# Weight sums of the second feed-forward layer: 28 pairs summed by VectorE in 8 KB rows in place of accumulating transfers

## The chip, the cores and the metric

The kernel runs on one core of a Trainium2 chip. The metric is the device time of one execution in microseconds (us). A run's time is the median of several executions; beside it stands one profiled execution, from which every row of a view below is taken. In those rows PE is TensorE, DVE is VectorE, ACT is ScalarE, POOL is GpSimd and SP is SyncE, which issues most of the transfers (SPq is its queue). L154 is line 154 of the kernel.

## What is computed

The reference is an encoder trunk of two layers on x of 256 positions by 2048 channels, all in float32. Layer 0 mixes by pooling and grouped-query attention, layer 1 by a bidirectional mLSTM of eight heads of width 256. Each layer then has a gated feed-forward part:

```python
def conv_ffn(x, w_up, conv_w, conv_b, w_down):
    u = x @ w_up                      # 256 x 2048 by 2048 x 11264
    up = jnp.pad(u, ((0, 0), (1, 1), (0, 0)))
    u = c[0] * up[:, :-2] + c[1] * up[:, 1:-1] + c[2] * up[:, 2:] + conv_b
    gate, val = jnp.split(u, 2, axis=-1)
    return (jax.nn.silu(gate) * val) @ w_down
```

The mLSTM layer projects x to queries, keys, values and an output gate (`h @ w_in`), computes for each head a 256 by 256 matrix of weighted scores, multiplies it with the values, and projects back with `w_out`.

## The kernel before

**The weight stream.** All weights pass through one stream (class `Stream`, L66 to L175) of 904 tiles of 128 partitions by 1024 floats, numbered from w0. The mLSTM layer's tiles are w404 to w565, the second feed-forward layer begins at w566. A tile is loaded by SP (`load`, L83; plain tiles at L100), then split into two float32r parts, high and low, called hl with the same number (`split`, L147): ScalarE copies the high part (L153) and VectorE subtracts it from the raw tile (L154). TensorE multiplies with high and low parts in three matmuls per product. Loads run six tiles ahead of TensorE in the mLSTM layer and eight in the feed-forward layers, splits three and four (`st.la`, `st.sa`). There are seven raw buffers and five split buffers: the load of a tile waits for the split of the tile seven before it, and a split waits until TensorE has done with the tile five before it.

**The order of work.** TensorE's program order is written by hand. The matrix products of the stream follow each other, and short tasks (`Weave`, L176) are put between them after a set amount of TensorE work. The other engines' order is made when the kernel is built: a scheduler puts their instructions in the order in which its own model of time has them ready; an instruction of an engine waits for those ahead of it on that engine.

**One head of the mLSTM** (`head`, L834) is such a task. VectorE prepares the gate matrix `arg` (L843), TensorE multiplies queries and keys into `qk`, VectorE multiplies the two (L856) and makes a divisor `denr` (L859 to L861), then four instructions write the matrix `A` (L863 to L866). TensorE transposes A (`atr`, L872), ScalarE and VectorE split the result into `at` (L874, L875), TensorE multiplies it with the values (`av`). The head's key tile is `hl_k` (L823), written by VectorE before `qk`.

**Summed weights.** Part of each up-projection is done with seven products of half-size blocks instead of eight, for units of four column tiles listed in `UNITS` (L1252). Those products need sums of weight blocks. For a pair of row tiles the four blocks b11, b12, b22, b21 lie side by side in DRAM, 512 floats each, 8 KB per partition in all. Four sums are made: s1 = b11 + b12, s2 = b12 + b22, s3 = b22 + s1, s4 = b21 + s3. A unit has eight pairs. The last number of its entry in `UNITS` is its kind. Kind 2, which most units have, makes s1, s3 and s4 ahead of time in a DRAM buffer G: SP copies blocks from DRAM to G (L122, L124), GpSimd issues transfers that add into G (L125 for s1, L129 for s3 and s4). s2 is then made by VectorE when the tile comes by (kind "left" of a tile, L141). Kind 1 makes all four ahead.

**When the sums are made.** `make_step` (L112) does one of four steps of a pair. `_make_steps` (L1339) gives each pair a place in the stream, "at", and a gap: step 0 comes right after the load of tile "at", step n after n gaps more. The second layer has 48 pairs, in the order of `UNITS`: 24 of the units (1,1), (2,1), (3,0), then those of (3,1), (4,1), (5,1). The first 28 pairs had these places (L1445), where `at` is 566:

```python
[(at - 240 + 11 * k, 5) for k in range(7)] + [(at - 162 + 38 * k // 5, 4) for k in range(21)]
```

Seven pairs were thus made during the first feed-forward layer, 21 during the mLSTM layer; the other 20 are made in the second feed-forward layer.

## Time and profile before

| | |
|---|---|
| median of 3 runs | 2157.26 us (2156.75 to 2157.31) |
| the profiled execution's own time | 2156.8 us |
| its span, first to last instruction | 2155.0 us |
| TensorE busy | 2148.3 us (100%) |
| VectorE busy | 1733.2 us (80%) |
| ScalarE busy | 1322.3 us (61%) |
| GpSimd busy | 301.7 us (14%) |
| SP's and ACT's transfers (queue q1) | 544.01 MB, 71.3% of 16 engines' time |
| GpSimd's transfers (queue q0) | 65.30 MB, 19.9% |

The median is 0.5 us above the profiled time, and the profiled time is 1.8 us above its span. A row of a timeline gives the start in us, the length in us, engine, line, operation, the tile written and the tiles read (without their numbers), a count where several equal instructions are merged, and in brackets how long the engine was idle before it and what released it.

### The profile page before, as it was taken

How to read it: one execution, taken by the hardware profiler on the slowest of the kernel's cores; microseconds unless marked ns; L12 is line 12 of the kernel's file. 1: busy time of each engine (PE TensorE's matmuls, PEld its weight loads, DVE VectorE, ACT ScalarE, POOL GpSimd, SP SyncE). 2: the span in 40 equal slices, each digit the busy share in tenths (PEclk: the TensorE clock that was granted, in tenths of full speed). 3: DMA queues.
4: the chain of work that ended last, by engine and by line, in shares of the span. 5: the costliest groups of instructions: out<-in, count | busy, mean ns of one | idle time of the engine just before them, and what ended most of it. 6: DMA issues, size and time to landing. Idle time of an engine off the chain costs nothing.

```text
span 2155.0 us, 31044 instructions
## 1 busy us (share of the span) xinstructions
PE 2148.3 (100%) x10824; PEld 1821.3 (85%) x10824; DVE 1733.2 (80%) x2417; ACT 1322.3 (61%) x1856; POOL 301.7 (14%) x376
## 2 busy tenths in 40 slices
PE   9999999999999999999999999999999999999999
PEld 8888888888888888889888888888888888888887
DVE  7686698989889787866777677669898979888985
ACT  7665566766557566656454544456676757675763
POOL 0222111111111111111111111111111111100000
PEclk9999999999999999999999999999999999999999
DMA  9989889999999999979898888888999999998773
GB/s 354 254 227 255 255 251 355 304 346 317 308 331 315 347 325 338 318 213 264 237 268 247 253 247 255 258 245 237 328 332 331 324 323 349 325 313 261 253 249 106
DMA packets 213727, 615.03 MB, mean 285 GB/s; under 512 B 27354, under 2 KB 29698, under 8 KB 213570
## 3 DMA queue, kind: packets, MB, share of 16 engines
q1 hardware_dynamic: 173216, 544.01, 71.3%
q0 software_dynamic: 37280, 65.30, 19.9%
q10 hardware_dynamic: 3074, 3.75, 0.7%
q8 instruction: 84, 1.38, 0.2%
q14 instruction: 73, 0.60, 0.1%
HBM read 610.81 MB, written 132.16 MB: 345 GB/s over the span
## 4 chain that ended last, share of the span: by engine, by line
PE 98%; DVE 1%; issue 0%; ACT 0%; DVEq 0%; ACTq 0%
PE up L282 22%; PE dn L282 22%; PE p L282 19%; PE op L282 8%; PE mv L282 4%; PE mq L282 4%; PE mk L282 4%; PE mo L282 4%; PE qproj L282 3%; PE pool L282 1%; PE kproj L282 1%; PE vproj L282 1%; PE tr L1097 1%; DVE hl L154 1%; PE av L282 1%; PE qk L282 1%
## 5 line engine op out<-in xcount | busy, mean ns | idle before, releaser
L154 DVE TENSOR_TENSOR hl<-w,hl 128x1024 fp32r<-128x1024 f32 (+1 forms) x904 | 1089.5, 1219 | 302.1 <-ACT hl L153 287.0
L153 ACT CAST hl<-w 128x1024 fp32r<-128x1024 f32 (+2 forms) x903 | 935.9, 1048 | 623.0 <-DVE w L141 105.2
L282 PE MATMUL up<-xx,hl 128*128 128x512 f32 (+1 forms) x2816 | 513.7, 337 | 0.0
L282 PEld LDWEIGHTS up<-xx,hl 128*128 128x128 f32 x2816 | 446.3, 188 | 70.4
L282 PE MATMUL dn<-hl,g 128*128 128x512 f32 x2064 | 492.1, 391 | 0.0
L282 PEld LDWEIGHTS dn<-hl,g 128*128 128x128 f32 x2064 | 385.3, 188 | 79.1
L282 PE MATMUL p<-hl,sx 128*128 128x512 f32 x1056 | 280.0, 390 | 0.2 <-DVE hl L154 0.2
L125 POOL DMA_DIRECT2D G<-in_q x176 | 148.1, 847 | 800.8 <-DMA G<-in_q 800.8
L282 PEld LDWEIGHTS p<-hl,sx 128*128 128x128 f32 x1056 | 193.6, 188 | 37.6 <-DVE hl L154 0.5
L129 POOL DMA_DIRECT2D G<-G x160 | 140.4, 882 | 605.4 <-DMA G<-in_q 266.8
L282 PE MATMUL p<-hl,xx 128*128 128x512 f32 x792 | 216.2, 390 | 0.0
L282 PEld LDWEIGHTS p<-hl,xx 128*128 128x128 f32 x792 | 144.6, 188 | 27.2
L282 PE MATMUL mk<-xx,hl 128*128 128x512 f32 (+1 forms) x512 | 92.2, 338 | 0.0
L282 PE MATMUL mq<-xx,hl 128*128 128x512 f32 (+1 forms) x512 | 92.2, 337 | 0.0
L282 PE MATMUL mv<-hl,xx 128*128 128x512 f32 (+2 forms) x480 | 91.8, 350 | 0.0
L282 PE MATMUL op<-hl,cat 128*128 128x512 f32 x384 | 91.6, 393 | 0.0
L282 PE MATMUL mo<-hl,xx 128*128 128x512 f32 x384 | 90.5, 391 | 0.0
L282 PE MATMUL op<-hl,mcat 128*128 128x512 f32 x384 | 89.5, 392 | 0.0
L282 PEld LDWEIGHTS mq<-xx,hl 128*128 128x128 f32 x512 | 79.3, 188 | 11.6
L282 PEld LDWEIGHTS mk<-xx,hl 128*128 128x128 f32 x512 | 79.1, 188 | 11.4
L282 PEld LDWEIGHTS mv<-hl,xx 128*128 128x128 f32 x480 | 78.3, 189 | 11.2
L282 PEld LDWEIGHTS op<-hl,mcat 128*128 128x128 f32 x384 | 71.5, 188 | 14.6
(242 smaller groups left out, 1877.8 us busy)
## 6 DMA issues: line engine op xcount, KB each, us to landing
w<-in_up SPq DMA_DIRECT2D x176, 512.0 KB, 6.6
w<-in_dn SPq DMA_DIRECT2D x176, 512.0 KB, 6.3
w<-in_m_in SPq DMA_DIRECT2D x124, 512.0 KB, 5.8
w<-in_q SPq DMA_DIRECT2D x96, 512.0 KB, 7.4
G<-in_q SPq DMA_DIRECT2D x160, 256.0 KB, 6.5
G<-G POOLq DMA_DIRECT2D x160, 256.0 KB, 7.4
w<-G SPq DMA_DIRECT2D x80, 512.0 KB, 7.2
w<-in_a_in SPq DMA_DIRECT2D x46, 512.0 KB, 6.5
```

Of the source, the lines that this page charges most:

```text
L125: pin(add.dma_start(G[r, 0:512], src[r, 512:1024], accum_op=ALU.add))
L129: pin(add.dma_start(G[:, at : at + 512], G[:, of : of + 512], accum_op=ALU.add))
L153: (self.nc.vector.tensor_copy if i + c == 0 else self.nc.scalar.copy)(hl[:, 0, c : c + n], w[:, c : c + n])
L154: self.nc.vector.tensor_sub(hl[:, 1, c : c + n], w[:, c : c + n], hl[:, 0, c : c + n].bitcast(F32))
L282: pe.matmul(out_, lhsT, rhs, start=start, stop=stop, skip_group_check=True)
L1097: pe.transpose(tr[:, j, t * P : t * P + P], src[:, c : c + P], ident)
```

## The change

Unit entries (1,1), (2,1) and (3,0) of the second layer become kind 1, so that s2 of their 24 pairs is made ahead too and no longer by VectorE when the tile comes by; that tile is then loaded in two halves, one from G and one from the weights. The first 28 pairs get a new kind 4, made in three steps: SP loads the pair's 8 KB rows (1 MB) into an SBUF room; one tile later VectorE makes the four sums in place; five or six tiles after the load SP stores the room (1 MB) to G. There are three rooms: two lie in the buffer that the mLSTM layer later uses as mcat1, one, gm, is new. The first 20 pairs take the rooms in turn, one pair every 4.25 tiles; the last eight pairs all use gm, one every eight tiles. All 28 pairs are made in the mLSTM layer. The memory set aside for GpSimd's transfers is halved, which makes place for gm.

```diff
         self.made, self.make, self.dpool = {}, make, dpool
+        self.rooms, self.room = [], {}
...
-        if part < 2:
+        if kind == 4:
+            if part == 0:
+                self.room[key] = self.rooms.pop(0)
+                pin(sync.dma_start(self.room[key], src))
+            elif part == 1:
+                w, sum_ = self.room[key], self.nc.vector.tensor_add
+                b11, b12, b22, b21 = (w[:, j * 512 : j * 512 + 512] for j in range(4))
+                pin(sum_(b11, b11, b12))
+                pin(sum_(b12, b12, b22))
+                pin(sum_(b22, b22, b11))
+                pin(sum_(b21, b21, b22))
+            else:
+                pin(sync.dma_start(G, self.room.pop(key)))
+        elif part < 2:
...
-            catb = [actp.tile([P, 8, 2, S], F32R, tag=f"B{i}", name=f"mcat{i}") for i in range(2)]
+            catb = []
+            gm = kp.tile([P, 2048], F32, tag="gm", name="gm")
+            gb = actp.tile([P, 2, 2048], F32, tag="B1", name="gb")
+            st.rooms = ([gb[:, 0], gb[:, 1], gm] * 7)[:20] + [gm] * 8
...
+                while len(catb) <= k // 8:
+                    catb.append(actp.tile([P, 8, 2, S], F32R, tag=f"B{len(catb)}", name=f"mcat{len(catb)}"))
+                    assert len(catb) < 2 or len(st.rooms) < 9
...
-    ((1, 1, 17, 37, 2), (2, 1, 38.5, 59, 2), (3, 0, 60, 79, 2), (3, 1, 80, 97, 2), (4, 1, 98.5, 121, 2),
+    ((1, 1, 17, 37, 1), (2, 1, 38.5, 59, 1), (3, 0, 60, 79, 1), (3, 1, 80, 97, 2), (4, 1, 98.5, 121, 2),
...
-    for (key, kind, q), (at, gap) in zip(pairs, places):
-        for part in range(4):
-            make.setdefault(at + part * gap, []).append((key, kind, part, q))
+    for (key, kind, q), (at, *gaps) in zip(pairs, places):
+        steps = [gaps[0] * part for part in range(4)] if len(gaps) == 1 else [0, *gaps]
+        for part, gap in enumerate(steps):
+            make.setdefault(at + gap, []).append((key, kind if len(gaps) == 1 else 4, part, q))
...
-    nc = _bacc.Bacc("TRN2", target_bir_lowering=False, num_devices=1, dynamic_dma_scratch_size=4096)
+    nc = _bacc.Bacc("TRN2", target_bir_lowering=False, num_devices=1, dynamic_dma_scratch_size=2048)
...
-    places.append([(at - 240 + 11 * k, 5) for k in range(7)] + [(at - 162 + 38 * k // 5, 4) for k in range(21)]
+    places.append([(at - 152 + 17 * k // 4, 1, 6) for k in range(20)] + [(at - 63 + 8 * k, 1, 5) for k in range(8)]
```

TensorE's order of instructions is the same in both kernels. On VectorE, ScalarE and SP the order changes, at many places of the mLSTM layer. Three of them follow; in the changed kernel all lines below the middle of `make_step` have higher numbers (L154 becomes L168, L859 becomes L879, L863 becomes L883).

The first place is VectorE at head 1. qk1, den1, denr1 and A1 are that head's tiles, hl437 to hl439 the split tiles of the stream, gb and gm the rooms. Before:

```order
L856 SCALAR_TENSOR_TENSOR arg1_9853,den1_9916<-qk1_9903,arg1_9853 128x128
L859 SCALAR_TENSOR_TENSOR denr1_9921<-den1_9916 128x4
L860 TENSOR_TENSOR denr1_9921<-denr1_9921,mc_9456 128x4
L861 RECIPROCAL denr1_9921<-denr1_9921 128x4
L863 TENSOR_SCALAR A1_9925<-arg1_9853,denr1_9921 128x256
L865 TENSOR_SCALAR A1_9925<-arg1_9853,denr1_9921 128x256
L864 SCALAR_TENSOR_TENSOR A1_9925<-arg1_9853,denr1_9921,A1_9925 128x128
L866 SCALAR_TENSOR_TENSOR A1_9925<-arg1_9853,denr1_9921,A1_9925 128x128
L154 TENSOR_TENSOR hl438_9974<-w438_9882,hl438_9974 128x1024
```

and in the changed kernel:

```order
L876 SCALAR_TENSOR_TENSOR arg1_9791,den1_9851<-qk1_9838,arg1_9791 128x128
L127 TENSOR_TENSOR gm_8968<-gm_8968 128x512
L126 TENSOR_TENSOR gb_8969<-gb_8969 128x512
L879 SCALAR_TENSOR_TENSOR denr1_9856<-den1_9851 128x4
L168 TENSOR_TENSOR hl438_9916<-w438_9821,hl438_9916 128x1024
L127 TENSOR_TENSOR gb_8969<-gb_8969 128x512
L880 TENSOR_TENSOR denr1_9856<-denr1_9856,mc_9387 128x4
L881 RECIPROCAL denr1_9856<-denr1_9856 128x4
L168 TENSOR_TENSOR hl439_9933<-w439_9865,hl439_9933 128x1024
L883 TENSOR_SCALAR A1_9860<-arg1_9791,denr1_9856 128x256
L885 TENSOR_SCALAR A1_9860<-arg1_9791,denr1_9856 128x256
L884 SCALAR_TENSOR_TENSOR A1_9860<-arg1_9791,denr1_9856,A1_9860 128x128
```

Before, the writes of A1 stood ahead of the splits hl438 and hl439; now both splits and three sums stand ahead of them.

The second place is VectorE at head 7, near the end of the layer. Before:

```order
L154 TENSOR_TENSOR hl533_12525<-w533_12440,hl533_12525 128x1024
L856 SCALAR_TENSOR_TENSOR arg7_12428,den7_12492<-qk7_12479,arg7_12428 128x128
L856 SCALAR_TENSOR_TENSOR arg7_12428,den7_12492<-qk7_12479,arg7_12428 128x256 x2
L856 SCALAR_TENSOR_TENSOR arg7_12428,den7_12492<-qk7_12479,arg7_12428 128x128
L859 SCALAR_TENSOR_TENSOR denr7_12497<-den7_12492 128x4
L860 TENSOR_TENSOR denr7_12497<-denr7_12497,mc_9456 128x4
L861 RECIPROCAL denr7_12497<-denr7_12497 128x4
L863 TENSOR_SCALAR A7_12501<-arg7_12428,denr7_12497 128x256
L865 TENSOR_SCALAR A7_12501<-arg7_12428,denr7_12497 128x256
L864 SCALAR_TENSOR_TENSOR A7_12501<-arg7_12428,denr7_12497,A7_12501 128x128
L866 SCALAR_TENSOR_TENSOR A7_12501<-arg7_12428,denr7_12497,A7_12501 128x128
L154 TENSOR_TENSOR hl534_12554<-w534_12462,hl534_12554 128x1024
```

and in the changed kernel, with the four sums of the 25th pair, the fifth that has gm alone:

```order
L168 TENSOR_TENSOR hl532_12461<-w532_12369,hl532_12461 128x1024
L124 TENSOR_TENSOR gm_8968<-gm_8968 128x512
L125 TENSOR_TENSOR gm_8968<-gm_8968 128x512
L168 TENSOR_TENSOR hl533_12482<-w533_12396,hl533_12482 128x1024
L876 SCALAR_TENSOR_TENSOR arg7_12384,den7_12443<-qk7_12430,arg7_12384 128x128
L876 SCALAR_TENSOR_TENSOR arg7_12384,den7_12443<-qk7_12430,arg7_12384 128x256 x2
L876 SCALAR_TENSOR_TENSOR arg7_12384,den7_12443<-qk7_12430,arg7_12384 128x128
L126 TENSOR_TENSOR gm_8968<-gm_8968 128x512
L879 SCALAR_TENSOR_TENSOR denr7_12448<-den7_12443 128x4
L127 TENSOR_TENSOR gm_8968<-gm_8968 128x512
L880 TENSOR_TENSOR denr7_12448<-denr7_12448,mc_9387 128x4
L168 TENSOR_TENSOR hl534_12507<-w534_12413,hl534_12507 128x1024
```

Two sums now stand ahead of hl533 and two among the small steps on denr7; hl534, which stood behind A7, stands ahead of it, and the four writes of A7 follow the last row.

The third place is SP's queue at the same time, with the loads of the stream's tiles w534 to w537. Before, pieces of a pair were copied to G behind them:

```order
L100 DMA w534_12462<-in_m_out 128x1024
L100 DMA w535_12506<-in_m_out 128x1024
L100 DMA w536_12523<-in_m_out 128x1024
L100 DMA w537_12548<-in_m_out 128x1024
L122 DMA G131_0_12443<-in_q1 64x512
L124 DMA G131_0_12443<-in_q1 64x1024
```

In the changed kernel the first row with gm stores the 24th pair and the second loads the 25th:

```order
L101 DMA w534_12413<-in_m_out 128x1024
L101 DMA w535_12457<-in_m_out 128x1024
L129 DMA G130_7_12208<-gm_8968 128x2048
L101 DMA w536_12476<-in_m_out 128x1024
L120 DMA gm_8968<-in_q1 128x2048
L101 DMA w537_12505<-in_m_out 128x1024
```

The store of one pair and the load of the next stand one tile apart and use the same room, so the load waits on SP until the store has landed, and w537 and all later tiles wait behind it.

## The prediction

> **What bounds the kernel now.** I read the page first: the span, the busy shares, and the chain that ended last.

> ```profile
> span 2155.0 us, 31044 instructions
> PE 2148.3 (100%) x10824; PEld 1821.3 (85%) x10824; DVE 1733.2 (80%) x2417; ACT 1322.3 (61%) x1856; POOL 301.7 (14%) x376
> PE 98%; DVE 1%; issue 0%; ACT 0%; DVEq 0%; ACTq 0%
> ```

> TensorE is busy in all but 6.7 us of the span, and the chain is TensorE's own work. Next I read everything TensorE waited for, and the place of the longest wait:

> ```profile
> PE tr L1097 <- DVE c L1074: 1.7, 1, 1.7
> PE wps L306 <- DVE pad L675: 1.2, 1, 1.2
> PE p L282 <- DVE hl L154: 0.2, 1, 0.2
> ...
> 1878.22 0.55 PE L1097 MATMUL tr<-cst,c 128*128 128x128 f32 x3 [1.66 <-DVE c L1074]
> ```

> Waits add up to 3.1 us. The change gives TensorE the same instructions in the same order, so nothing that it takes off another engine can return more than 3.1 us; about 4.3 us, 0.2%, is what a measurement of this kernel can tell from no change. The question is whether it makes TensorE wait where it does not now. For that I read the busy time by stage:

> ```profile
> 977.00:1411.00 434.00, 434.00 (x2342) 374.13 (x2341) 304.73 (x476) 224.19 (x305) 70.09 (x87) 1.00 0.89 254
> ...
> 1600.00:1700.00 100.00, 100.00 (x503) 84.72 (x502) 91.32 (x121) 69.84 (x93) 13.02 (x16) 1.00 0.99 324
> ```

> The columns are stretch, length, then busy us of PE, PEld, DVE, ACT and POOL, the granted clock, the DMA share and GB/s. In the mLSTM layer, 977 to 1411, VectorE is busy 304.73 of 434 us, 70%; in the second feed-forward layer 91%, with TensorE still never idle, so 90% of VectorE alone is no harm. The order of its work has to do the harm, if any is done.

> **What the change removes.** GpSimd's accumulating transfers for 28 pairs go, and 24 sums (s2) in the feed-forward layer.

> ```profile
> L141 DVE TENSOR_TENSOR w<-w 128x512 f32<-128x512 f32 x88 | 60.4, 686 | 0.0
> ACT hl L153 <- DVE w L141: 105.2, 55, 3.4
> POOL G L125 <- DMA G<-in_q: 800.8, 140, 15.3
> ```

> 24 sums by 686 ns are 16.5 us of VectorE; ScalarE's casts wait for such sums, but no wait of TensorE ends on one. GpSimd sits idle for 800.8 us for transfers and no row of TensorE names it. I cost this at nothing on the path. It could at most take away the wait at 1878.22, which belongs to unit (3,1), of unchanged kind; I leave it in.

> **What it adds: work.** 28 pairs by 4 sums by 686 ns are 76.9 us of VectorE, all in the mLSTM layer. Over its 434 us that lifts the 70% by 17.7 points to 88%, under the 91% above. The transfers of the same stretch, by queue and by tile (the last column is from issue to landing):

> ```profile
> q1 hardware_dynamic: 27354, 92.41, 60.5%
> q0 software_dynamic: 8784, 15.47, 25.8%
> w<-in_m_in SPq DMA_DIRECT2D x116, 512.0 KB, 5.9
> ...
> G<-in_q SPq DMA_DIRECT2D x38, 256.0 KB, 6.2
> ...
> G<-in_q SPq DMA_DIRECT2D x38, 128.0 KB, 5.9
> ```

> q0's 25.8% (112 us) nearly all goes. q1 moves 92.41 MB in 60.5% of 434 us, 352 GB/s. 28 loads and 28 stores of 1.05 MB are 58.7 MB, 167 us at that rate; the copies that they replace (38 of 256 KB and 38 of 128 KB, 14.9 MB, 42 us at that rate) go. In all 167 - 42 - 112 = 13 us are added to 434: the share of the transfers hardly moves. A weight tile lands 5.9 us after issue and is issued six tiles, some 16 us, ahead.

> **What it adds: order.** TensorE stops at a head's four transposes (L872) until VectorE has written A. The rows of before at head 1:

> ```profile
> 1054.08 0.35 DVE L863 TENSOR_SCALAR A<-arg,denr 128x256 f32<-128x256 f32 x1
> 1054.87 0.35 DVE L866 SCALAR_TENSOR_TENSOR A<-arg,denr,A 128x128 f32<-128x128 f32 x1
> 1056.68 0.60 PE L872 MATMUL atr<-cst,A 128*128 128x128 f32 x4
> 1056.88 1.05 ACT L153 CAST hl<-w 128x1024 fp32r<-128x1024 f32 x1 [1.62 <-PE mo L282]
> 1057.97 1.23 DVE L154 TENSOR_TENSOR hl<-w,hl 128x1024 fp32r<-128x1024 f32 x1
> ```

> The four writes take 1.14 us (1054.08 to 1055.22), 1.5 us ahead of the transposes. In the changed order the split hl439 stands ahead of them: it is the last row. It cannot start sooner, since its cast at 1056.88 waited for TensorE to give up a buffer. So it ends at 1059.20, the writes (each follows 0.08 before the last one's end) at 1060.3, and the transposes due at 1056.68 wait **3.6 us**. The three sums there (1.8 us) hide ahead of the cast. If the pair's load is late, more comes on top.

> Head 5 has the same change, by one split:

> ```profile
> 1245.88 1.06 ACT L153 CAST hl<-w 128x1024 fp32r<-128x1024 f32 x1 [3.13 <-PE mo L282]
> 1246.97 1.23 DVE L154 TENSOR_TENSOR hl<-w,hl 128x1024 fp32r<-128x1024 f32 x1
> 1248.11 1.40 DVE L843 SCALAR_TENSOR_TENSOR arg<-G,mc,kml 128x128 f32<-128x128 f32 x4
> 1248.36 0.60 PE L872 MATMUL atr<-cst,A 128*128 128x128 f32 x4
> ```

> hl502 ends at 1248.20 whatever stands before, A5 1.06 later at 1249.26 where 1248.36 is due: **0.9 us**.

> Head 0 waits on its key tile hl_k, which `qk` reads:

> ```profile
> 1016.76 0.69 DVE L447 TENSOR_TENSOR tb_k<-mk,tb_k 128x512 f32<-128x512 f32 x1 [0.31 <-ACT tb_k L446]
> 1019.23 0.68 DVE L823 TENSOR_TENSOR hl_k<-tb_k,hl_k 128x512 fp32r<-128x512 f32 x1
> 1022.91 1.60 PE L282 MATMUL qk<-hl_k,hl_q 128*128 128x256 f32 x12
> ```

> Four sums (0.61 apart, 2.4) and four steps on `arg` (1.4, as at 1248.11) now stand ahead of it, less 0.3 of idle time: 1019.91 becomes 1023.4, **0.5 us** late (0 to 1.1). Heads 2, 3, 4 and 6 I find hidden.

> Head 7 hangs on a transfer. Its rows, with SP's issues of w535 and w536:

> ```profile
> 1326.30 0.33 SPq L100 DMA_DIRECT2D w<-in_m_out  x1
> 1328.90 0.33 SPq L100 DMA_DIRECT2D w<-in_m_out  x1
> ...
> 1339.76 0.28 DVE L856 SCALAR_TENSOR_TENSOR arg<-qk,arg 128x128 f32<-128x128 f32 x1
> 1342.39 0.35 DVE L866 SCALAR_TENSOR_TENSOR A<-arg,denr,A 128x128 f32<-128x128 f32 x1
> 1342.81 1.22 DVE L154 TENSOR_TENSOR hl<-w,hl 128x1024 fp32r<-128x1024 f32 x1
> 1344.20 0.60 PE L872 MATMUL atr<-cst,A 128*128 128x128 f32 x4
> ...
> out<-x SPq DMA_DIRECT2D x3, 512.0 KB, 3.1
> DMA to landing us min/median/max: 8.4/8.6/8.8
> ```

> The store of pair 24 is issued behind w535, at 1326.6; the load of pair 25, in the same room gm, waits on SP for its landing. With Ls and Ll for the two landings and 0.4 for each issue, the pair is there at X = 1327.4 + Ls + Ll. Then its four sums (2.4), two splits (1.14 each, 2.3) and head 7's steps from the first product to the last write of A (1339.76 to 1342.74, 3.0) run in one row, 7.7 us. Where the landings are short, the split hl534 (last DVE row) decides as at head 5, and A7 is some 1.1 us late. The trace has no 1 MB transfer. From below: 5 us each, 10 together, gives an end of 1345.1, 0.9 late and under that floor: 1.1 us. From above: 9 each, a little over the 8.4 to 8.8 of the two weight tiles w535 and w536 issued here, gives 1353.1, 8.9 late. I take the load as the 5.9 of half the size plus 1.5 (0.52 MB at 352 GB/s), 7.4; the store as 3.1 plus 1.5, plus 1.5 for the weight tile ahead of it in the queue, 6.1; together 13.5, nearer the lower end because most rows of this layer are. X is 1340.9, A7 is done at 1348.6, **4.4 us** late.

> [...]

> Sum: 3.6 + 0.9 + 0.5 + 4.4 = 9.4 us. The span becomes 2164.4, the profiled time 1.8 more, 2166.2, the median 0.5 more: **2166.7 us**. Lower bound: 3.6 + 0.9 + 0 + 1.1 = 5.6, a median of 2162.9.

> **Rivals.** *The stalls are absorbed.* If VectorE reaches A1 and A5 before the splits' buffers come free, or SP's queue runs so far ahead that gm is never waited for, TensorE stays full. For: 88% is under the 91% that does no harm. Against: VectorE takes its instructions in the order shown, and the row at 1056.88 holds hl439 back by TensorE's own pace. It decides whether A1 is written by 1056.68. Then the median is 2157, or 2155.4 with the wait at 1878.22 gone.

> *The queue becomes the bound.* Loads and stores of 1 MB stand in SP's queue ahead of weight tiles; at 9 us a landing the wait for gm (18.8 us with two issues) plus sums and splits between them, about 6, is 25 us for a pair, where eight tiles take 21.4 (434 us by 8/162). Three pairs follow on gm, each 3.6 us later than the last, and the weight loads behind them come as late. 3.6 + 0.9 + 0.5 + 8.9 + 10.8 is 24.7 us, a median of 2182 (2155.0 + 24.7 + 1.8 + 0.5). It decides from about 7.2 us a landing (half of the 3.6 between 25 and 21.4, under 9). For: 8.8 us occurs here already, at half the size. Against: accumulating traffic leaves q0. [...]

> *The smaller memory waits.* Should the smaller memory for GpSimd's transfers make it wait, its remaining pairs come late; few of them are under way at once, so I give this nothing of its own.

> **Numbers.** The forecast 0.60, absorbed 0.20 (0.03 of it with the last wait gone by enough to be faster by over 0.2%, though 3.1 us scarcely allows it), the queue 0.20. Slower by over 0.2% means above 2161.6, and both other cases lie there; same holds the rest of absorbed and 0.01 from the forecast's edge. The range runs from 2157, the absorbed case, to 2178, which leaves out the upper half of the queue's case and the gains.

> **What would show it.** TensorE's waits in the new profile should name A (L883 to L886) at L892's transposes in three heads: 3.6, 0.9 and about 4 us near 1344; `qk` for hl_k at 0.5; and SP waiting for G's store ahead of the loads into gm. VectorE's sum should read 112 by 0.69 us. No wait at head 1 proves the first term wrong; a wait on weight tiles (hl) instead of A proves the queue's case; a time under 2158 proves the whole sum wrong.

## The result, and the profile after

The changed kernel takes 2166.09 us (median of 5 runs, 2165.67 to 2166.88), the kernel before 2156.75 us (median of 5, 2156.69 to 2157.31): the ratio is 1.0043, with a 95% interval from 1.0030 to 1.0056. The forecast was 2166.7. The total fits; the parts fit less well. The profiled execution is the longest of the five, 2166.88, so its rows explain 10.1 us and not 9.3. Its mean granted clock is 0.998; that of the other four is 0.999.

The first lines of the changed kernel's page:

```profile
span 2165.1 us, 30906 instructions
PE 2152.3 (99%) x10824; PEld 1822.8 (84%) x10824; DVE 1785.8 (82%) x2505; ACT 1323.2 (61%) x1856; POOL 211.3 (10%) x264
```

The span is 10.1 us longer. TensorE, with the same instructions, is busy 4.0 us longer than before, and the rest is waiting. What it waited for (total, times, longest), and where, from its timeline:

```profile
PE atr L892 <- DVE A L884: 4.8, 3, 3.2
PE tr L1117 <- DVE c L1094: 1.7, 1, 1.7
...
PE cols L296 <- ACT rows_b L819: 1.1, 1, 1.1
```

```profile
1004.98 0.64 PE L296 MATMUL cols<-cst,rows_b 40*128 40x40 f32 x4 [1.05 <-ACT rows_b L819]
1063.17 0.72 PE L892 MATMUL atr<-cst,A 128*128 128x128 f32 x4 [3.18 <-DVE A L884]
1257.12 0.66 PE L892 MATMUL atr<-cst,A 128*128 128x128 f32 x4 [0.52 <-DVE A L884]
1354.21 0.66 PE L892 MATMUL atr<-cst,A 128*128 128x128 f32 x4 [1.07 <-DVE A L884]
```

Heads 1, 5 and 7 wait for A, as forecast; the wait of `cols` at the layer's start is new and was not forecast. The windows of the layer, and of the two stretches in which the granted clock (third column from the right) is not 1.00:

```profile
977.00:1421.00 444.00, 438.18 (x2344) 376.68 (x2343) 367.77 (x584) 224.04 (x306) 7.09 (x9) 0.99 0.85 308
1005.61:1009.02 3.41, 3.41 (x11) 2.91 (x11) 3.09 (x4) 3.04 (x5) 0.00 (x0) 0.50 0.85 339
1063.63:1067.04 3.41, 3.41 (x10) 2.73 (x9) 1.79 (x5) 1.43 (x2) 0.00 (x0) 0.50 1.01 419
```

Behind two of the four waits TensorE ran at half clock for 3.41 us. That is the longer busy time: 3.41 at 0.50 loses 1.7 us, twice 3.4 of the 4.0. Most of the rest I call the restart, some 0.2 us at each wait (the remainders in the table below). Rows of full matmuls overlap, those of `mo` for example are 0.39 us long and start 0.23 apart; a wait is counted from the end of the last row, and the overlap that it takes away counts as busy.

Two such stretches take 0.16% off the mean clock, which is the profiled execution's 0.998. At 0.999 the other four executions lost less than that, so the median's 9.3 us need not have the same parts as the 10.1 below; no trace shows them.

Where the 10.1 us lie is read by setting the start of one instruction in both traces side by side: `qk` of head 0 and `av` of heads 1, 5 and 7. Of the kernel before (its `qk` row stands in the prediction):

```profile
1061.25 1.59 PE L282 MATMUL av<-mvt,at 128*128 128x256 f32 x12
...
1252.93 1.59 PE L282 MATMUL av<-mvt,at 128*128 128x256 f32 x12
...
1348.77 1.59 PE L282 MATMUL av<-mvt,at 128*128 128x256 f32 x12
```

and of the changed kernel:

```profile
1026.04 1.62 PE L296 MATMUL qk<-hl_k,hl_q 128*128 128x256 f32 x12
...
1069.39 1.58 PE L296 MATMUL av<-mvt,at 128*128 128x256 f32 x12
...
1261.76 1.59 PE L296 MATMUL av<-mvt,at 128*128 128x256 f32 x12
...
1358.82 1.59 PE L296 MATMUL av<-mvt,at 128*128 128x256 f32 x12
```

They lie 3.1, 8.1, 8.8 and 10.05 us later. So:

| place | lost, us | wait | restart and half clock |
|---|---|---|---|
| start of the kernel, before the layer | 0.3 | | |
| layer's start, `cols` | 2.8 | 1.05 | 1.75 |
| head 1 | 5.0 | 3.18 | 1.8 |
| head 5 | 0.7 | 0.52 | 0.2 |
| head 7 | 1.2 | 1.07 | 0.2 |

After head 7 the shift stays at 10.1 to the end. (The 0.3 is in place 13 us into the kernel, long before the first sum; in the runs below it comes and goes by a few tenths.)

What stands behind the `cols` wait, from the changed kernel's chain of waits (first row) and VectorE's timeline:

```profile
978.40 13.09 DMA gb<-in_q
...
991.51 0.69 DVE L124 TENSOR_TENSOR gb<-gb 128x512 f32<-128x512 f32 x1 [5.07 <-DMA gb<-in_q]
992.12 0.48 DVE L800 TENSOR_SCALAR pre<-gtr,kml 104x256 f32<-104x256 f32 x1
```

The second pair's load took 13.1 us to land. VectorE had reached that pair's first sum and stood still for 5.07 us, and behind the sum, in VectorE's order, stands `pre`, the first step of the gates, from which a chain of small steps on VectorE and ScalarE leads to `cols`. In the kernel before `pre` ran at 986.04:

```profile
986.04 0.48 DVE L780 TENSOR_SCALAR pre<-gtr,kml 104x256 f32<-104x256 f32 x1
```

It ran 6.1 us later now, more than the chain had to spare.

Some loads by tile (count, KB, median us to landing; gb's loads and stores, not shown, took 8.8 and gm's stores 6.0), the sums left in the feed-forward layers, and ScalarE's waits for them:

```profile
w<-in_m_in SPq DMA_DIRECT2D x116, 512.0 KB, 6.3
w<-in_m_out SPq DMA_DIRECT2D x30, 512.0 KB, 4.4
...
gm<-in_q SPq DMA_DIRECT2D x14, 1024.0 KB, 6.4
```

```profile
L155 DVE TENSOR_TENSOR w<-w 128x512 f32<-128x512 f32 x64 | 43.9, 686 | 0.0
ACT hl L167 <- DVE w L155: 79.3, 42, 3.4
```

24 sums are gone there and ScalarE waits 25.9 us less for them; TensorE's wait in that layer (`tr` for c, 1.7 us) is what it was.

### The profile page after: what moved, and what is told of

Its sections match the earlier page's. It is cut to its first block, busy times and chain, and to the rows that moved or that the text cites. A ratio compares the mean times of both kernels' runs of the same rounds, so it can differ in the third digit from the quotient of the medians.

```text
span 2165.1 us, 30906 instructions
## 1 busy us (share of the span) xinstructions
PE 2152.3 (99%) x10824; PEld 1822.8 (84%) x10824; DVE 1785.8 (82%) x2505; ACT 1323.2 (61%) x1856; POOL 211.3 (10%) x264
## 4 chain that ended last, share of the span: by engine, by line
PE 94%; DVE 2%; DMA 2%; issue 1%; ACT 1%; SPq 0%; ACTq 0%; DVEq 0%
PE dn L296 22%; PE up L296 21%; PE p L296 19%; PE op L296 8%; PE mk L296 4%; PE mq L296 4%; PE mv L296 3%; PE mo L296 3%; PE qproj L296 3%; DVE hl L168 1%; PE pool L296 1%; PE vproj L296 1%; PE tr L1117 1%; PE kproj L296 1%; DMA gb<-in_q 1%
## 5 line engine op out<-in xcount | busy, mean ns | idle before, releaser
L168 DVE TENSOR_TENSOR hl<-w,hl 128x1024 fp32r<-128x1024 f32 (+1 forms) x904 | 1091.7, 1219 | 267.1 <-ACT hl L167 250.1
L139 POOL DMA_DIRECT2D G<-in_q x120 | 100.3, 838 | 590.1 <-DMA G<-in_q 589.8
L143 POOL DMA_DIRECT2D G<-G x104 | 89.1, 856 | 462.5 <-DMA G<-in_q 181.2
L296 PEld LDWEIGHTS mo<-hl,xx 128*128 128x128 f32 x384 | 72.2, 191 | 14.6
## 6 DMA issues: line engine op xcount, KB each, us to landing
w<-in_up SPq DMA_DIRECT2D x176, 512.0 KB, 6.6
w<-in_dn SPq DMA_DIRECT2D x176, 512.0 KB, 6.0
w<-in_m_in SPq DMA_DIRECT2D x124, 512.0 KB, 6.3
w<-G SPq DMA_DIRECT2D x80, 512.0 KB, 7.3
w<-in_q SPq DMA_DIRECT2D x72, 512.0 KB, 7.3
w<-in_q SPq DMA_DIRECT2D x112, 256.0 KB, 6.7
w<-G SPq DMA_DIRECT2D x112, 256.0 KB, 6.8
G<-in_q SPq DMA_DIRECT2D x104, 256.0 KB, 7.4
```

What stands on the lines that cost most here:

```text
L139: pin(add.dma_start(G[r, 0:512], src[r, 512:1024], accum_op=ALU.add))
L143: pin(add.dma_start(G[:, at : at + 512], G[:, of : of + 512], accum_op=ALU.add))
L168: self.nc.vector.tensor_sub(hl[:, 1, c : c + n], w[:, c : c + n], hl[:, 0, c : c + n].bitcast(F32))
L296: pe.matmul(out_, lhsT, rhs, start=start, stop=stop, skip_group_check=True)
```

## The experiments

Theory: what costs is the order on VectorE, which puts sums and splits ahead of short chains that TensorE waits for; a wait costs its length, 0.2 us of restart, and sometimes 1.7 us at half clock. Rival: what costs is the load, VectorE's some 60 us more of work in the layer (367.77 us in the window above, 304.73 before) or the 1 MB transfers in SP's queue, and waits only move if the order is mended. All are compared with runs of the kernel before on the same chip (2156.8 us in both groups).

**Sums behind A.** In `head` the last of A's four writes is noted, and a pair's first sum may not be issued on VectorE ahead of it:

```diff
+                st.behind = v.scalar_tensor_tensor(A[:, 1, P:S], ..., ALU.mult, ALU.add).ins
...
-                pin(sum_(b11, b11, b12))
+                with self.tc.issue_after(self.behind) if self.behind else nullcontext():
+                    pin(sum_(b11, b11, b12))
```

> Same work, places and rooms as the changed kernel; a pair's first sum may not be issued on VectorE ahead of the newest head's four writes of A. Theory (order): the stalls come from what stands ahead of A on VectorE, and a stall costs its wait plus up to 1.8 us at half clock behind it. Head 1 then waits 0.4 us at most in place of 3.2 and its half clock goes (5.0 to 0.4), heads 5 and 7 do not wait (0.7 and 1.3 gone); the wait of cols for rows_b at the layer's start stays with its half clock (2.8). 2166.1 - 4.6 - 2.0 = 2159.5 us, up to 1 us more if a head's later steps come late behind the moved sums. Rival (load): VectorE at 88% and 1 MB transfers in SP's queue cost the time, the wait only moves: 2165 to 2167.

Measured: 2159.92 us, ratio 1.0013 (1.0005 to 1.0022). The waits for A are gone, `cols` still waits:

```profile
PE cols L297 <- ACT rows_b L820: 1.4, 1, 1.4
```

With the work unchanged, 6.2 us come back by order alone (2166.09 less 2159.92). The load as the cause falls, for the larger part.

**Other places.** The sums unhindered, the pairs elsewhere:

```diff
-    places.append([(at - 152 + 17 * k // 4, 1, 6) for k in range(20)] + [(at - 63 + 8 * k, 1, 5) for k in range(8)]
+    places.append([(at - 150 + 17 * k // 4, 3, 7) for k in range(20)] + [(at - 61 + 8 * k, 1, 5) for k in range(8)]
```

> The changed kernel with other places only: the first 20 pairs two tiles later, sums three tiles after the load, not one, stores seven, not six; the last eight pairs two tiles later. Theory (order): the first sums now come behind the gate's steps or find their data landed, so the wait of cols and its half clock go (2.8); heads 5 and 7 have no sum ahead of A (2.0 gone); at head 1 two sums and both splits hl438 and hl439 still stand ahead of A, so about 3.0 us and 1.8 of half clock stay (5.0 to 4.8); head 3 gets 0.7 with a sum behind its split. 2166.1 - 2.8 - 2.0 - 0.2 + 0.7 = 2161.8 us. Rival (load): the same work in the same layer, 2165 to 2167.

Measured: 2160.28 us, ratio 1.0019 (1.0010 to 1.0027). The profiled execution:

```profile
PE atr L892 <- DVE A L884: 2.7, 1, 2.7
...
PE atr L892 <- DVE A L886: 0.3, 1, 0.3
```

`cols`, head 5 and head 7 wait no more; head 1 waits 2.7 us and head 3, with a sum behind its split, 0.3, not 0.7. The median is 1.5 below what was expected. The profiled execution has no half clock behind head 1: its span is 2158.4, 3.4 above before, of which the two waits (2.9) and two restarts (0.4) make 3.3. The 11 times of this kernel lie in two groups, six from 2159.99 to 2160.28 and five from 2161.58 to 2161.87, 1.6 us apart: about what 3.41 us at half clock cost, and the upper group is where 2161.8 was expected. The mean granted clock is 1.000 in each of the six and 0.999 in each of the five. My estimate from these figures is that the same kernel meets the half clock in some executions and not in others; a trace exists of one of them.

**Both.** The places of the second, the order of the first:

> The places of the second kernel of this call and the sums held behind A as in the first. Same VectorE work, same transfers. Theory (order): no wait of TensorE is left but those of the kernel before: 2156.8 us, at most 1 above. Rival (load): over 2161, since nothing is taken away.

Measured: 2156.80 us (2156.68 to 2156.96 in 11 runs), ratio 0.9999 (0.9990 to 1.0008).

```profile
span 2155.0 us, 30915 instructions
...
PE tr L1118 <- DVE c L1095: 1.7, 1, 1.7
PE wps L321 <- DVE pad L690: 1.2, 1, 1.2
PE p L297 <- DVE hl L169: 0.2, 1, 0.2
...
977.00:1411.00 434.00, 434.00 (x2342) 374.30 (x2341) 366.67 (x584) 223.73 (x305) 9.79 (x9) 1.00 0.87 316
```

The waits are those of the kernel before, and so is the span, with VectorE at 366.67 of 434 us and 1 MB transfers in the same number. This decides it: the work and the traffic that the change adds cost nothing where they stand so. All of the 9.3 us came from order, on VectorE and in the places of the pairs. The traffic is no lighter: the longest landing of the pairs' loads is 13.9 us here, 14.4 in the changed kernel, but VectorE stood still for gb's loads only once, for 0.7 us.

**Kind 1 alone.** The kernel before with the three units as kind 1, their sums still made by GpSimd's transfers in the old places:

```diff
-    ((1, 1, 17, 37, 2), (2, 1, 38.5, 59, 2), (3, 0, 60, 79, 2), (3, 1, 80, 97, 2), (4, 1, 98.5, 121, 2),
+    ((1, 1, 17, 37, 1), (2, 1, 38.5, 59, 1), (3, 0, 60, 79, 1), (3, 1, 80, 97, 2), (4, 1, 98.5, 121, 2),
```

> The kernel before with one part of the change alone: the three units are kind 1 (their s2 made ahead, by GpSimd's transfers; 24 sums fewer on VectorE in the second feed-forward layer), old places, no sums by VectorE in the mLSTM layer. Prediction's term: worth nothing, 2156.8 us. Rival: VectorE runs ahead in the feed-forward layer and the 1.7 us wait of tr for c goes: 2155.1 us.

Measured: 2160.36 us, ratio 1.0015 (1.0006 to 1.0024): both guesses missed. TensorE has new waits, all ahead of or at head 0 but for a 0.4 us one at 896; the last two rows are VectorE's timeline and the chain of waits at that place:

```profile
PE mq L282 <- DVE tb_q L447: 1.0, 1, 1.0
PE qk L282 <- DVE hl_k L823: 0.7, 1, 0.7
...
1015.78 1.14 DVE L843 SCALAR_TENSOR_TENSOR arg<-G,mc,kml 128x256 f32<-128x256 f32 x3 [2.18 <-DMA G<-gd]
...
1005.08 10.61 DMA G<-gd
```

VectorE stands at head 0's `arg`, with splits and `tb_q` behind it, until the gates' rows land, 10.6 us after issue. It is the same pattern as at the layer's start above: an early-placed step on VectorE waits for a transfer that is late there. That the larger copies of kind 1 (512 KB, not 256 and 128) are what made it late was not tried. The `tr` wait stays at 1.7, so the lighter VectorE in the feed-forward layer gains nothing, as forecast.

**Waits by design.** Two kernels ask which waits are followed by the half clock. They are the kernel before, with less of TensorE's work between `qk` and the transposes of A, by other amounts in each head:

```diff
-                yield 5.0
+                yield [1.8, 2.0, 2.2, 1.0, 1.8, 2.0, 1.0, 1.0][h]
```

(in the second kernel 1.0, 1.0, 1.8, 2.0, 1.0, 1.0, 2.2, 2.0).

> The kernel before with one thing changed: in each head less of TensorE's work stands between qk and the transposes of A, so that TensorE must wait for A by design; the sums and transfers are those of before. By the rows of before (A done 1.3 us ahead of the transposes in even heads, 1.5 in odd ones; 0.23 us a matmul of mo, 0.17 of mq) the waits should be near 2.2, 1.3, 1.5, 2.7, 2.2, 1.3, 2.9 and 2.7 us in heads 0 to 7, 16.8 in all, and 0.2 us each for the restart. What is asked: which of them is followed by 3.4 us at half clock (1.7 more). [...] Rival (length): each wait over about 1 us is followed by it, wherever it falls: 8 times 1.7. Total: 2156.8 + 16.8 + 1.6 + 1.7 for each: 2178 to 2189 us.

> As the kernel before it in this call, with the lengths dealt out otherwise: waits near 2.9, 2.7, 2.2, 1.3, 2.9, 2.7, 1.5 and 1.3 us in heads 0 to 7 (17.5 in all). [...] 2179 to 2190 us.

Measured: 2174.25 and 2175.68 us, ratios 1.0082 (1.0067 to 1.0098) and 1.0086 (1.0072 to 1.0100), both below the range given: the waits came out shorter, 12.5 and 13.2 us in all. But they are of few lengths, which serves the question. Of the first, its two longest waits (heads 3 and 7) and windows behind them:

```profile
1155.19 0.66 PE L872 MATMUL atr<-cst,A 128*128 128x128 f32 x4 [2.24 <-DVE A L864]
...
1355.05 1.11 PE L872 MATMUL atr<-cst,A 128*128 128x128 f32 x4 [2.24 <-DVE A L864]
...
1155.50:1159.00 3.50, 3.50 (x19) 2.91 (x18) 1.96 (x6) 2.48 (x3) 0.00 (x0) 1.00 0.57 200
1354.99:1358.40 3.41, 3.35 (x10) 2.86 (x11) 0.96 (x3) 0.59 (x1) 0.00 (x0) 0.50 0.41 123
```

Two waits of the same 2.24 us: one is followed by the half clock, one is not. Length alone is refuted. Of the second, waits in heads 1, 4 and 5 and the windows of half clock:

```profile
1057.77 0.66 PE L872 MATMUL atr<-cst,A 128*128 128x128 f32 x4 [2.24 <-DVE A L864]
1228.86 0.55 PE L872 MATMUL atr<-cst,A 128*128 128x128 f32 x3 [1.40 <-DVE A L864]
1259.24 0.66 PE L872 MATMUL atr<-cst,A 128*128 128x128 f32 x4 [2.24 <-DVE A L864]
...
1058.82:1062.23 3.41, 3.41 (x10) 2.63 (x9) 1.73 (x4) 2.11 (x3) 0.00 (x0) 0.50 0.38 46
1260.20:1263.62 3.42, 3.42 (x10) 2.65 (x9) 1.65 (x5) 2.21 (x3) 0.00 (x0) 0.50 0.17 50
```

Here both waits of 2.24 us are followed by the half clock, for 3.41 and 3.42 us, and the one of 1.40 is not: the 16 matmuls of `mq` behind it take 3.04 us, as they do in head 0, where the granted clock from 1029 to 1033 is 1.00. Nor is the 1.65 us that `tr` waits in the changed kernel, up to 1888.29: the clock from 1888.30 to 1891.70 is 1.00.

**Other places** has a longer wait without the half clock, at head 1 of its profiled execution:

```profile
1059.54 0.66 PE L892 MATMUL atr<-cst,A 128*128 128x128 f32 x4 [2.66 <-DVE A L884]
1059.96 4.36 PE L296 MATMUL mo<-hl,xx 128*128 128x512 f32 x18
```

The 18 matmuls of `mo` behind this wait take 4.36 us, and 4.37 behind the wait that ends at 1155.19, at 1.00; behind the two waits of 2.24 us in the second kernel they take 5.97 and 5.98. What decides beside the length is not shown by these runs.

**Both, and a later `tr`.** The kernel of **Both**, with one wait of the kernel before taken away as well:

```diff
-                            wv.add(finish(c12, c22, fs[2:], gt, i0 + 2, name), 3.0)
+                            wv.add(finish(c12, c22, fs[2:], gt, i0 + 2, name), 4.8 if layer else 3.0)
```

> The kernel with other places and the sums held behind A, and in the second feed-forward layer the first transposes of a unit's result stand 4.8 us of TensorE's work behind the unit's last product, not 3.0. The one wait of TensorE there, tr for c, 1.7 us in the kernel before as well, should go, since c is written 1.2 us after the old place: 2156.8 - 1.7 - 0.2 = 2154.9 us. Rival: with tr later, the steps behind it come late for the next unit or the down-projection, and the wait moves: 2156.8 or more.

Measured: 2154.94 us, ratio 0.9993 (0.9984 to 1.0002). `tr` is no longer among TensorE's waits:

```profile
PE wps L321 <- DVE pad L690: 1.2, 1, 1.2
PE kproj L297 <- ACT xx L360: 0.3, 1, 0.3
```

The interval reaches just past 1, but ten of the 11 times (2154.69 to 2155.08; one is 2158.74) lie under the lowest of 15 of before, 2156.56. It is 1.8 us, close to the 1.9 worked out, and below both kernels. The wait that it takes away is as long in the kernel before; whether that kernel would gain as much from a later `tr` was not run.

## Why the prediction was right in total, point by point

*What bounds it, and what the removal is worth.* Right. TensorE's own work bounds every one of these kernels, no wait of TensorE ended on the parts removed, and with order mended the time is that of before to 0.1 us.

*The added work and traffic cost nothing.* Right (**Both**). VectorE rose to 84% in the layer, not 88%: 62 us more (366.67 less 304.73), mostly since one pair falls outside the stretch and consecutive rows overlap by 0.08.

*Head 1, 3.6 us.* The mechanism was right, the wait 3.18. The split hl439 starts at 1061.10, its old 1057.97 plus the shift of 3.1, and the writes follow it:

```profile
1061.10 1.23 DVE L168 TENSOR_TENSOR hl<-w,hl 128x1024 fp32r<-128x1024 f32 x1 [0.55 <-ACT hl L167]
...
1062.77 0.35 DVE L884 SCALAR_TENSOR_TENSOR A<-arg,denr,A 128x128 f32<-128x128 f32 x1
```

TensorE starts on the third write, L884, as its waits say, 0.26 us ahead of the fourth that the sum used. *Head 5, 0.9*: for the same reason 0.52.

*Head 0's key tile, 0.5.* No wait, but only just:

```profile
1025.33 0.68 DVE L843 TENSOR_TENSOR hl_k<-tb_k,hl_k 128x512 fp32r<-128x512 f32 x1
```

hl_k ends at 1026.01, 0.03 ahead of `qk` at 1026.04. It is 6.1 us later than before and TensorE itself, from `cols`, 3.1; the 3.0 left use up what there was to spare, where the sum took 3.5. In **Other places** and **Both**, four sums stand ahead of hl_k as well, but the steps on `arg` are done earlier, and hl_k ends 1.6 and 0.4 us ahead of `qk`.

*Head 7, 4.4 us.* This step failed by its size: 1.07. SP waited for the store and the load followed, as said:

```profile
1336.01 0.33 SPq L129 DMA_DIRECT2D G<-gm  x1
...
1342.06 0.33 SPq L120 DMA_DIRECT2D gm<-in_q  x1
...
1346.95 0.69 DVE L124 TENSOR_TENSOR gm<-gm 128x512 f32<-128x512 f32 x1 [1.08 <-DMA gm<-in_q]
```

From the end of each issue (0.33) the store took about 5.7 us and the load 4.6: 10.3 together, not the 13.5 that I took. That is close to the lower bound, where the split hl534 sets a floor of 1.1 us. Its cast ended at 1351.57 on ScalarE (1350.51 and 1.06), and the split followed the last sums:

```profile
1351.94 1.22 DVE L168 TENSOR_TENSOR hl<-w,hl 128x1024 fp32r<-128x1024 f32 x1
```

So the pair in gm held the split back by some 0.4 us, and the rest of the 1.07 is the split's own place ahead of A7, as at head 1. The transfer, named as what head 7 hangs on, was the lesser part. The load was the term most off, 4.6 for 7.4: I took 5.9 for half its size from the input projections' tiles, where the output projection's, beside which it ran, now took 4.4. What the size itself adds is not settled: at the median 1 MB took 6.0 to 8.8 us over the layer.

*What was not in the sum.* The `cols` wait: I costed moved steps where they stood ahead of A and of `hl_k`, but did not follow `pre` and its chain, though the order shows a sum there, and took every early load as landed. And what follows a wait: half clock and restart, 1.75 + 1.8 + 0.2 + 0.2 or 4.0 us in all. The two omissions (2.8 with its half clock, 2.2 behind the heads) nearly equal what was put too high (3.3 at head 7, 0.8 at heads 1 and 5, 0.5 at hl_k). So the total of 9.4 against the median's 9.3 is in part luck: with its own terms sized as they were measured in the profiled execution it would have been 4.8, below the lower bound of 5.6.

*The rivals.* Absorbed: not in this kernel, but **Both** shows that the order and the places were all it lacked. The queue as the bound: no wait of TensorE names a weight tile that was late, and the tiles of the input projections land in 6.3 us (5.9 before), those of the output projection in 4.4 (5.9 before); refuted. The smaller memory for GpSimd's transfers: without effect, since **Both** has it as well.

Open: why the loads issued at 978.4 and 986.9 took 13.1 and 14.4 us, the one at 967.7 only 5.2 and later ones 4.9 to 11.8 was not tried.

## What to carry to other kernels

VectorE had time to spare in the layer (busy 304.73 of 434 us), and 62 us of new work on it were free here only where they did not stand ahead of the short chains on which TensorE waits: follow each of these chains in the new order, not only the busiest ones, and give each transfer that a queued step waits for its latest landing, not its median (13.1 us at `pre`, where the median of gb's loads was 8.8). With the sums held behind the heads' chains and placed three tiles behind their load, not one, the same work cost nothing here; each of the two alone left 3.1 and 3.5 us.
